# A two-layer hybrid decoder step on one core: the low halves of the second layer's input weights computed on VectorE instead of GpSimd

## The chip, the cores and the metric

The kernel runs on one core of one Trainium2 chip. The metric is the device time of one execution in microseconds (us), the median of three runs. A profile is one further execution, taken by the hardware profiler. Engines are called as the profile calls them: PE is TensorE (matmuls; PEld its weight loads), DVE is VectorE, ACT is ScalarE, POOL is GpSimd, SP is SyncE, which issues all DMAs here. L92 is line 92 of the kernel.

## The reference, cut to what matters

One inference step of a decoder trunk with two layers, for 1024 prompt tokens and 8 sample tokens that share all weights, in float32, model width 1024. The first layer (attention and a state-space scan) is not touched. The second is an mLSTM layer with 8 heads of width 256:

```python
def odd_layer(hn, w_in, w_out, conv_w, conv_b, ig_b, fg_b, norm_w, conv_buf, c0, n0, m0):
    u = hn @ w_in
    q_pre, k_pre, v, o_pre, i_pre, f_pre, z = _split(u, ODD_SPLITS)
    qk, new_conv = causal_conv(jnp.concatenate([q_pre, k_pre], axis=-1), conv_buf, conv_w, conv_b)
    ...
    i_t = i_pre.astype(jnp.float32) + ig_b.astype(jnp.float32)
    logf = jax.nn.log_sigmoid(f_pre.astype(jnp.float32) + fg_b.astype(jnp.float32))
    h, c, n, m = mlstm_chunked(q, k, v, i_t, logf, c0, n0, m0)
    h = jax.nn.sigmoid(o_pre.astype(jnp.float32)).reshape(b, L, MLSTM_HEADS, MLSTM_HD) * h
    h = head_norm(h, norm_w).reshape(b, L, MLSTM_INNER).astype(hn.dtype)
    out = (h * jax.nn.silu(z)) @ w_out
    return out, new_conv, c, n, m
```

`mlstm_chunked` runs over chunks of 128 tokens. For the 8 sample tokens the same layer updates 8 large state matrices (one step each).

## The kernel before, in words

A float32 product is made of three matmuls of a faster 32-bit type (`mm3`, L113): every operand x is split into a high half, which ScalarE casts (`split`, L91), and a low half x minus high, which is one subtraction (L92) on an engine that the call names: `V` is VectorE, `G` is GpSimd. Activations are split once (tiles `yh`, `yl` in the second layer). Weights are split as they stream in: `raw_load` (L96) brings a 128x1024 block from memory into one of three `raw` buffers, `wsplit` makes `wh` and `wl`, or `wvh` and `wvl`, from it.

Two queues of weights feed the second layer's heads:

- `wq1`, a `Weights` object: 48 blocks, six a head, four for q and k and two for the gate z. `next` hands out one block and fetches (cast and subtraction) the next. Its high and low halves have two buffers each, so the cast of a block waits until TensorE has finished the block two places before it. `first` names the engines of the first subtractions, `engs` those of the rest, in turn.
- `wv_fetch`: 32 blocks, four a head, for v and o, which lie ready for the whole head.

A head runs so. For each of the four q and k blocks `conv_c` makes three chunks of 344 columns, 24 matmuls each, in PSUM (`pf`, three banks), and ScalarE copies each out (L238, L240). Then comes the convolution (`conv_taps`: L244 on ScalarE, three L246 on VectorE) and, one block later, its activation (`conv_act`: L250 on ScalarE, L251 on VectorE). For the two z blocks `gate_c` empties a bank with a copy and a tanh on ScalarE (L231, `gth` L232), and VectorE multiplies (L233, `msz`). Between the blocks stand the sample tokens' convolution (L265 to L270 and L277 on VectorE, `csy` and `cst`; L276 on ScalarE) and, from head 2 on, steps of the state update for the sample tokens of the two heads before: a load of `dC` (L1345), a scaling on ScalarE (L1394), then in turn four L1398 (`dC`) and four L1402 (`dnum`) on VectorE, and a store (L1403). An even head has three such steps, an odd head seven. After the z blocks follow nine `vo_block`s with the chunks of the mLSTM (`ml_prep`, `ml_main`, `ml_out`), in which GpSimd has work of its own (`mE`, `mqq`, `mql`, `mCl`, `md`).

In head 0 a chain for the gates runs beside the projections: `lf` and the matmul `pbc` (L1177), a running maximum in seven pairs of steps (`gp`, L1191 and L1192) and the transpose `pgl` (L1197), a recurrence over the eight chunks (`mp`, L1199 and L1200) and the matmul `pmb` (L1207).

After the heads comes the output projection (`wqf`, matmul L927), whose blocks are split on VectorE and GpSimd in turn.

The order of instructions on each engine is set by a scheduler when the program is built; each engine then works through its queue in that order, and one that waits holds up all behind it.

Of the kernel before, what the change touches and what calls it, by code (L numbers as in the profile page):

```python
# [7 lines left out]
F32R = mybir.dt.float32r  # L8
# [21 lines left out]
def body(ctx, tc, I, O):  # L30
    nc = tc.nc
    V, A, G, PE = nc.vector, nc.scalar, nc.gpsimd, nc.tensor
# [4 lines left out]
    def pool(name, bufs=1, stack=ctx, **kw):  # L37
        return stack.enter_context(tc.tile_pool(name=name, bufs=bufs, **kw))
# [18 lines left out]
    def S(name, dt=F32):  # L57
        return cur["slab"].tile([128, 1040], dt, tag="S", name=name)
# [31 lines left out]
    def split(hi, lo, src, eng=V):  # L90
        A.copy(hi, src)  # L91
        eng.tensor_tensor(lo, src, hi.bitcast(F32), sub)  # L92

    def raw_load(src, n):
        raw = rawp.tile([128, 1040], F32, tag="raw", name="raw")
        load(raw[:, :n], src)  # L96
        return raw

    def wsplit(src, n, th, tl, eng=V, raw=None):
        raw = raw_load(src, n) if raw is None else raw  # L100
        split(th[:, :n], tl[:, :n], raw[:, :n], eng)
        return th, tl
# [1006 lines left out]

    layer1 = scope("1", SLABS1)  # L1110
    cur["w"] = pool("wp1", 2, layer1)
    wq1 = Weights([(I[n_][h, j], 1024) for h in range(8) for n_, cnt in (("wq", 4), ("wz", 2)) for j in range(cnt)], (G,), (V, V))

    gb = C("gb", [128, 16], I["gb"].partition_broadcast(128))
    wgr = TMP("wgr")[:, :128].rearrange("p (a b) -> p a b", b=16)
# [315 lines left out]
    wvr = deque()  # L1431

    wvraw = deque()

    def wv_load():
        if wvp and not wvraw:
            wvraw.append(raw_load(I["wvo"][wvp[0][0], wvp[0][1]], 1024))

    def wv_fetch(n):
        for _ in range(n):  # L1440
            wv_load()
            wvp.popleft()
            wvr.append(wsplit(None, 1024, S("wvh", F32R), S("wvl", F32R), G, wvraw.popleft()))

    def vo_block(hd, c, wv):
        p = MM("pvo")
# [49 lines left out]
    for h in range(8):  # L1496
# [3 lines left out]
        for j in range(4):  # L1500
# [24 lines left out]
            if j == 2:  # L1525
                wv_load()
        hd["q"], hd["k"] = qk[0:2], qk[2:4]
        wv_fetch(2)
        hist = SM("mhist", [128, 4, 3, 8], 1)
        load(hist, I["mch"][:, 4 * h : 4 * h + 4])  # L1530
        smp = conv_sample_taps(mxs, hist, mcw[:, 4 * h : 4 * h + 4], mcb[:, 4 * h : 4 * h + 4], 4, O["mconvs"][:, 4 * h : 4 * h + 4])
        hd["z"] = []
        for j in range(2):
            w = wq1.next()
            t2 = S("msz")
            for c in range(3):
                gate_c(w, xh, xl, c, t2[:, c * CH : (c + 1) * CH])
                if j == 0 and c == 2:
                    t = conv_sample_act(*smp)
                slot(c)  # L1540
            A.copy(szs[:, 2 * h + j], t2[:, NP:T])
            hd["z"].append(t2)
            wv_fetch(1)
            if h2 or j == 0:
                pump(1)
# [299 lines left out]
```

## Time and profile before

| | us |
|---|---|
| median of three runs | 2216.33 (2213.23 to 2218.28) |
| the profiled execution | 2213.76 |
| its span, first to last instruction | 2211.7 |
| granted TensorE clock, mean over the span | 0.986 |
| busy PE, DVE, ACT, POOL | 2117.2, 1381.0, 845.4, 857.7 |
| the second layer's heads | about 836 to 2004 of the span |
| the output projection and final norm | 2004 to the end |

Busy time of PE is not PE at its peak: matmuls are pipelined, and at half clock they are busy twice as long. In a row of waits stand the waiting instruction, what ended the wait, the total, the number and the longest. In a timeline row stand start, length and instruction, and in brackets the engine's idle time before it.

### The profile page before, as it was taken

Reading aid. Unit: us, or ns where it says so; the run is one execution under the profiler, and the core shown is the slowest. Engines: PE = TensorE matmul, PEld = TensorE weight load, DVE = VectorE, ACT = ScalarE, POOL = GpSimd, SP = SyncE. Lnnn points to the kernel's source line nnn. Section 1 sums busy time; section 2 is a strip of 40 time slices with the busy share of each in tenths; the row PEclk is TensorE's granted clock in tenths of the full one; section 3 lists DMA queues with packets and bytes.
Section 4 is the critical chain, followed back from the end, with each engine's and each line's share of the span. In section 5 each row is a group of like instructions: output and inputs, shape, how many; then the busy total and the mean of one; then the engine's idle time right before and its main releaser. Section 6 shows DMA issues by size and latency. Waiting matters only on the chain. (4 is left out here: it accounts for less than half of the span.)

```text
span 2211.7 us, 35220 instructions
## 1 busy us (share of the span) xinstructions
PE 2117.2 (96%) x12913; PEld 1890.8 (85%) x12913; DVE 1381.0 (62%) x3075; ACT 845.4 (38%) x1828; POOL 857.7 (39%) x1167
## 2 busy tenths in 40 slices
PE   7999989998999999899999999999999999999998
PEld 6877777997898798789988889898898988987798
DVE  7344488678877545644648566576575664856854
ACT  5434434454434323433424334243343342523331
POOL 4222152115543343343444435434354344542321
PEclk9999999999999999999999999999999999999999
DMA  4222142325555551411213223132241232415753
GB/s 156 70 73 76 52 145 73 93 71 174 166 183 185 159 175 40 94 37 48 88 33 109 77 89 123 36 102 82 75 138 28 84 104 61 139 38 187 256 179 101
DMA packets 161918, 232.29 MB, mean 105 GB/s; under 512 B 41170, under 2 KB 106690, under 8 KB 161746
## 3 DMA queue, kind: packets, MB, share of 16 engines
q1 hardware_dynamic: 161746, 230.04, 33.2%
q8 instruction: 102, 1.67, 0.3%
q14 instruction: 70, 0.57, 0.1%
HBM read 174.35 MB, written 55.62 MB: 104 GB/s over the span
## 5 line engine op out<-in xcount | busy, mean ns | idle before, releaser
L113 PE MATMUL pf<-yh,wh 128*128 128x344 f32 x1152 | 375.5, 326 | 11.9 <-ACT gth L232 11.0
L113 PE MATMUL pf<-yl,wh 128*128 128x344 f32 x1152 | 372.7, 323 | 1.7 <-POOL yl L92 1.7
L113 PE MATMUL pf<-yh,wl 128*128 128x344 f32 x1152 | 371.5, 323 | 0.3 <-DVE wl L92 0.3
L92 POOL TENSOR_TENSOR wl<-raw,wh 128x1024 fp32r<-128x1024 f32 x86 | 214.6, 2495 | 353.6 <-ACT wh L91 353.6
L113 PEld LDWEIGHTS pf<-yh,wh 128*128 128x128 f32 x1152 | 219.6, 191 | 16.6 <-ACT gth L232 13.5
L113 PEld LDWEIGHTS pf<-yl,wh 128*128 128x128 f32 x1152 | 219.6, 191 | 2.6 <-POOL yl L92 2.6
L113 PEld LDWEIGHTS pf<-yh,wl 128*128 128x128 f32 x1152 | 219.2, 190 | 0.8 <-DVE wl L92 0.7
L246 DVE SCALAR_TENSOR_TENSOR cout<-craw,mcw,cout 128x1024 f32<-128x1024 f32 x96 | 145.7, 1518 | 114.7 <-ACT cout L244 113.1
L91 ACT CAST wh<-raw 128x1024 fp32r<-128x1024 f32 x128 | 134.1, 1048 | 207.6 <-PE po L927 82.0
L113 PE MATMUL pvo<-wvh,yh 128*128 128x512 f32 x512 | 205.8, 402 | 0.0
L113 PE MATMUL pvo<-wvl,yh 128*128 128x512 f32 x512 | 201.7, 394 | 0.0
L113 PE MATMUL pvo<-wvh,yl 128*128 128x512 f32 x512 | 201.6, 394 | 0.0
L113 PE MATMUL pf<-xh,wh 128*128 128x344 f32 x576 | 195.8, 340 | 2.7 <-ACT gth L232 2.7
L113 PE MATMUL pf<-xl,wh 128*128 128x344 f32 x576 | 188.0, 326 | 0.0
L113 PE MATMUL pf<-xh,wl 128*128 128x344 f32 x576 | 187.7, 326 | 0.0
L1263 DVE TENSOR_SCALAR mx<-mx,mbs,md 128x256 f32<-128x256 f32 x64 | 26.4, 413 | 178.0 <-POOL md L1262 178.0
L927 PE MATMUL po<-oh,wl 128*128 128x512 f32 (+2 forms) x384 | 123.6, 322 | 5.2 <-DVE wl L92 4.2
L927 PE MATMUL po<-oh,wh 128*128 128x512 f32 (+2 forms) x384 | 123.9, 324 | 1.0 <-ACT oh L91 1.0
L927 PE MATMUL po<-ol,wh 128*128 128x512 f32 (+2 forms) x384 | 123.1, 321 | 0.0
L113 PEld LDWEIGHTS pf<-xh,wh 128*128 128x128 f32 x576 | 110.8, 192 | 8.8 <-issue 4.9
L92 POOL TENSOR_TENSOR wvl<-raw,wvh 128x1024 fp32r<-128x1024 f32 x32 | 85.5, 2674 | 78.1 <-ACT wvh L91 78.1
L113 PEld LDWEIGHTS pvo<-wvh,yl 128*128 128x128 f32 x512 | 96.1, 188 | 22.3
(435 smaller groups left out, 5307.0 us busy)
## 6 DMA issues: line engine op xcount, KB each, us to landing
raw<-in_wo SPq DMA_DIRECT2D x56, 512.0 KB
raw<-in_wq SPq DMA_DIRECT2D x32, 512.0 KB
raw<-in_wvo SPq DMA_DIRECT2D x32, 512.0 KB
dC<-in_mcs SPq DMA_DIRECT2D x32, 512.0 KB
out_mcs<-dC SPq DMA_DIRECT2D x32, 512.0 KB
raw<-in_wf SPq DMA_DIRECT2D x24, 512.0 KB
sE<-acd SPq DMA_DIRECT2D x16, 512.0 KB
raw<-in_wz SPq DMA_DIRECT2D x16, 512.0 KB
```

The source lines that it names most:

```text
L91: A.copy(hi, src)
L92: eng.tensor_tensor(lo, src, hi.bitcast(F32), sub)
L113: PE.matmul(out, l, r, start=i == 0, stop=i == n - 1)
L246: V.scalar_tensor_tensor(o[:, :NP], raw[:, j : j + NP], w4[:, j : j + 1], o[:, :NP], mult, add)
L927: PE.matmul(p[:, :m], wt[:, ws], at, start=i == 0 and q == 0, stop=i == nk - 1 and q == 2)
L1263: V.tensor_scalar(x, x, bs[:, 6:7], d[:, 2:3], sub, mult)
```

## The change

The subtractions of the low halves of `wq1` and of the value weights name VectorE. The first two of `wq1` did so before; 46 of `wq1` and 32 of `wv_fetch` move. The output projection's blocks (`wqf`) still take VectorE and GpSimd in turn.

```diff
     cur["w"] = pool("wp1", 2, layer1)
-    wq1 = Weights([(I[n_][h, j], 1024) for h in range(8) for n_, cnt in (("wq", 4), ("wz", 2)) for j in range(cnt)], (G,), (V, V))
+    wq1 = Weights([(I[n_][h, j], 1024) for h in range(8) for n_, cnt in (("wq", 4), ("wz", 2)) for j in range(cnt)], (V,))
...
         for _ in range(n):
             wv_load()
             wvp.popleft()
-            wvr.append(wsplit(None, 1024, S("wvh", F32R), S("wvl", F32R), G, wvraw.popleft()))
+            wvr.append(wsplit(None, 1024, S("wvh", F32R), S("wvl", F32R), V, wvraw.popleft()))
```

The scheduler places the moved subtractions in VectorE's queue and moves some neighbours. First place: VectorE in head 4, at the fourth k block, where the sample convolution (L268 to L277) stands ahead of the first z block; + is after, - before.

```order
+L92 TENSOR_TENSOR wl<-raw,wh 128x1024
 L268 TENSOR_TENSOR cst<-mxs,mcw 128x32
 L269 TENSOR_TENSOR csy<-csy,cst 128x32
 L270 TENSOR_TENSOR csy<-csy,mcb 128x32
 L246 SCALAR_TENSOR_TENSOR cout<-craw,mcw,cout 128x1024
+L92 TENSOR_TENSOR wvl<-raw,wvh 128x1024
+L246 SCALAR_TENSOR_TENSOR cout<-craw,mcw,cout 128x1024
+L92 TENSOR_TENSOR wvl<-raw,wvh 128x1024
+L246 SCALAR_TENSOR_TENSOR cout<-craw,mcw,cout 128x1024
+L233 SCALAR_TENSOR_TENSOR msz<-gth,msz 128x344 x2
 L277 SCALAR_TENSOR_TENSOR cst<-cst,csy 128x32
```

The weight's subtraction comes ahead of L268, and two value subtractions come between the three L246 of that block; the other q and k blocks have their subtraction ahead of their three L246.

Second place: ScalarE in the same stretch of head 1, at the first z block (the other heads up to 6 read alike).

```order
 L232 ACTIVATE gth<-pf 128x344
-L250 ACTIVATE craw<-cout 128x1024
-L231 COPY msz<-pf 128x344
-L232 ACTIVATE gth<-pf 128x344
-L91 CAST wvh<-raw 128x1024
+L231 COPY msz<-pf 128x344
+L232 ACTIVATE gth<-pf 128x344
+L91 CAST wvh<-raw 128x1024
+L250 ACTIVATE craw<-cout 128x1024
 L91 CAST wh<-raw 128x1024
```

L250, which waits for the third L246 on VectorE, now comes behind the second copy and tanh of the z block.

Third place: VectorE in head 0, inside the running maximum `gp`.

```order
+L92 TENSOR_TENSOR wl<-raw,wh 128x1024
 L1191 TENSOR_TENSOR gp<-gp 64x124
 L1192 COPY gp<-gp 64x4
-L268 TENSOR_TENSOR cst<-mxs,mcw 128x32
+L246 SCALAR_TENSOR_TENSOR cout<-craw,mcw,cout 128x1024
 L1191 TENSOR_TENSOR gp<-gp 64x120
 L1192 COPY gp<-gp 64x8
-L269 TENSOR_TENSOR csy<-csy,cst 128x32
+L246 SCALAR_TENSOR_TENSOR cout<-craw,mcw,cout 128x1024
```

A subtraction and three L246 (before, these stood behind or at the end of `gp`) come into the chain, and a value subtraction ahead of its last pair. On TensorE the transpose `pgl` stands 5 matmuls later than before, and `pmb` 57 matmuls behind `pgl` instead of 31.

## The prediction

> **What bounds the kernel now.** I read the page first, then the windows of the second layer's part, the waits of TensorE there, the groups of VectorE and GpSimd, and last the timeline at the longest waits. Page, the busy row:
>
> ```profile
> PE 2117.2 (96%) x12913; PEld 1890.8 (85%) x12913; DVE 1381.0 (62%) x3075; ACT 845.4 (38%) x1828; POOL 857.7 (39%) x1167
> ```
>
> TensorE is the bound. The windows (columns: stretch, length, busy of PE, PEld, DVE, ACT, POOL, granted clock, DMA share, GB/s) give the eight heads of the second layer, one heavy and one light slice of them, and four stretches at half clock:
>
> ```profile
> 836.00:2004.00 1168.00, 1135.74 (x6653) 1032.16 (x6653) 712.82 (x1653) 434.51 (x900) 522.71 (x780) 0.99 0.25 78
> 1480.00:1500.00 20.00, 17.69 (x101) 17.12 (x101) 18.16 (x21) 11.28 (x18) 9.95 (x5) 0.91 0.36 119
> 1940.00:1960.00 20.00, 20.00 (x109) 16.87 (x108) 9.63 (x37) 6.36 (x18) 6.59 (x15) 1.00 0.07 18
> 912.30:915.70 3.40, 2.99 (x11) 2.88 (x12) 3.40 (x7) 0.33 (x1) 0.28 (x1) 0.51 0.43 154
> 922.60:929.40 6.80, 4.29 (x16) 4.14 (x17) 3.45 (x21) 1.06 (x4) 0.20 (x1) 0.50 0.37 129
> 1492.60:1496.00 3.40, 3.40 (x14) 3.40 (x13) 3.40 (x3) 0.00 (x0) 2.36 (x1) 0.50 0.05 8
> 1779.30:1782.70 3.40, 3.40 (x14) 3.40 (x13) 3.40 (x4) 0.07 (x1) 0.83 (x1) 0.50 0.85 306
> ```
>
> TensorE is short of work for 32 of the 1168 us, and where it is, VectorE is nearly full (18.16 of 20). So TensorE's time can only fall by its waits and by the half clock behind them. Its waits in that part (total, times, longest):
>
> ```profile
> PE pf L113 <- ACT gth L232: 11.0, 9, 2.2
> PE pmb L1207 <- DVE mp L1200: 5.8, 1, 5.8
> PE pgl L1197 <- DVE gp L1191: 3.4, 1, 3.4
> PE pbc L1177 <- DVE lf L295: 1.2, 1, 1.2
> PE pf L113 <- ACT craw L238: 1.0, 2, 0.8
> ```
>
> These 22.4 us come from VectorE: directly in the gate chain (mp, gp, lf: 10.4), and through ScalarE in the projections (12.0), because ScalarE's queue stands still on VectorE's results before it empties a PSUM bank. The timeline at the first wait of 2.2 us (start, length, instruction; brackets: idle before):
>
> ```profile
> 1197.71 2.40 POOL L92 TENSOR_TENSOR wl<-raw,wh 128x1024 fp32r<-128x1024 f32 x1 [5.66 <-ACT wh L91]
> 1197.76 2.63 DVE L1402 SCALAR_TENSOR_TENSOR dnum<-dC,dq,dnum 128x256 f32<-128x256 f32 x1
> 1200.31 3.04 DVE L1398 SCALAR_TENSOR_TENSOR dC<-dvb,dkw,dC 128x256 f32<-128x256 f32 x2
> 1200.45 2.62 POOL L92 TENSOR_TENSOR wvl<-raw,wvh 128x1024 fp32r<-128x1024 f32 x1
> 1204.63 0.19 DVE L270 TENSOR_TENSOR csy<-csy,mcb 128x32 f32<-128x32 f32 x1
> 1204.86 0.23 ACT L276 ACTIVATE cst<-csy 128x32 f32<-128x32 f32 x1 [4.62 <-DVE csy L270]
> 1206.78 0.43 PE L113 MATMUL pf<-yh,wh 128*128 128x344 f32 x1 [2.23 <-ACT gth L232]
> ```
>
> A VectorE instruction of half a microsecond lasts 2.6 us, as long as the GpSimd subtraction that it meets. That is the rule, not this spot: the groups (count, busy, mean ns) and, behind them, min/median/max ns of the same instructions:
>
> ```profile
> L92 POOL TENSOR_TENSOR wl<-raw,wh 128x1024 fp32r<-128x1024 f32 x47 | 117.3, 2496 | 155.3 <-ACT wh L91 155.3
> L92 POOL TENSOR_TENSOR wvl<-raw,wvh 128x1024 fp32r<-128x1024 f32 x32 | 85.5, 2674 | 78.1 <-ACT wvh L91 78.1
> L246 DVE SCALAR_TENSOR_TENSOR cout<-craw,mcw,cout 128x1024 f32<-128x1024 f32 x96 | 145.7, 1518 | 114.7 <-ACT cout L244 113.1
> L1402 DVE SCALAR_TENSOR_TENSOR dnum<-dC,dq,dnum 128x256 f32<-128x256 f32 x93 | 67.3, 724 | 0.7
> L1398 DVE SCALAR_TENSOR_TENSOR dC<-dvb,dkw,dC 128x256 f32<-128x256 f32 x96 | 64.1, 701 | 13.5 <-ACT dC L1394 13.2
> L233 DVE SCALAR_TENSOR_TENSOR msz<-gth,msz 128x344 f32<-128x344 f32 x48 | 50.9, 1063 | 40.4 <-ACT gth L232 40.4
> ```
> ```profile
> L246 DVE SCALAR_TENSOR_TENSOR cout<-craw,mcw,cout x96: 1270/1285/3498, 872.6 to 1920.4; 128x1024 f32<-128x1024 f32 x96
> L1402 DVE SCALAR_TENSOR_TENSOR dnum<-dC,dq,dnum x93: 469/480/2664, 1170.5 to 1916.8; 128x256 f32<-128x256 f32 x93
> L1398 DVE SCALAR_TENSOR_TENSOR dC<-dvb,dkw,dC x96: 469/480/2652, 1169.1 to 1913.8; 128x256 f32<-128x256 f32 x96
> L233 DVE SCALAR_TENSOR_TENSOR msz<-gth,msz x48: 471/516/2749, 915.2 to 1936.9; 128x344 f32<-128x344 f32 x48
> L92 DVE TENSOR_TENSOR wl<-raw,wh x3: 1203/1214/1218, 837.1 to 1927.8; 128x1024 fp32r<-128x1024 f32 x3
> ```
>
> **The change part by part.** Taken off GpSimd: 46 subtractions of projection weights (one of the 47 above is the output projection's and stays) at 2.496 us and 32 of value weights, 85.5 us: 200 us. It was no bound (523 of 1168 us busy), so this alone gives nothing.
>
> Put on VectorE: 78 subtractions at 1.214 us, 94.7 us. Given back there, mean minus median times count: L246 22.4, L1402 22.7, L1398 21.2, L233 26.3, together 92.6 us, and some 11 us more from five small gate instructions, each held about 2.2 us:
>
> ```profile
> 903.49 2.59 DVE L1192 COPY gp<-gp 64x8 f32<-64x8 f32 x1
> 906.11 2.62 DVE L1191 TENSOR_TENSOR gp<-gp 64x112 f32<-64x112 f32 x1
> 910.30 2.35 DVE L1191 TENSOR_TENSOR gp<-gp 64x64 f32<-64x64 f32 x1
> 918.21 2.32 DVE L1200 TENSOR_TENSOR mp<-mp,btot 1x8 f32<-1x8 f32 x1
> 920.75 2.07 DVE L1200 TENSOR_TENSOR mp<-mp,btot 1x8 f32<-1x8 f32 x1
> ```
>
> VectorE's load so stays where it is (about -9 us); what changes is where its time falls. A subtraction now stands directly behind the cast that it needs and ahead of the three L246, which wait for ScalarE's L244 (113.1 us of idle time): it fills a pause where VectorE is early.
>
> Whether TensorE then waits for the subtraction itself: the weight is needed one weight later, 72 matmuls (three chunks of 24) after the cast may start; the chain has a stretch without a wait:
>
> ```profile
> 1868.37 18.75 PE pf L113 x119
> ```
>
> That is 0.157 us for one, 11.3 us for 72; cast and subtraction take 2.3. VectorE may be 9 us behind before it costs anything. Queued behind the waiting subtraction are L246 and the dC steps; SyncE waits for it too, since the raw buffer is then free for the next load, which comes sooner by 1.2 us where VectorE is not late. DMA counts do not change.
>
> Projection waits, at 1204: 2.15 us of L1402 and 2.16 of the two L1398 go, 1.21 is added, so L270 ends 3.1 us earlier than the 2.2 us wait needs. Moreover L250, on which ScalarE also stood, is now behind the second gth. I take 9 of the 12.0 us.
>
> Gate chain: between the start of gp and its end 6.8 us of holding go, and two subtractions and three L246 come in (2.4 + 3.9): 0.5 us earlier, and TensorE asks for it 5 matmuls (0.8 us) later. The mp chain loses 4.1 us of holding and, ahead of it, two L246, and gets two subtractions and one L233; it ends some 3 us earlier, and TensorE asks 31 matmuls (4.9 us) later. I take 7 of the 10.4 us: pmb nearly all, pgl 1.3, pbc the rest.
>
> Half clock: in the four stretches TensorE is busy 14.1 us at half speed, so 7.0 us are lost; each comes shortly after a wait. I take 4. By the Trainium skill, "TensorE: Matmul & The Clock Gate", section "Why this matters for your kernels", the clock drops after TensorE gaps above about 3 us; the trace does not agree for 1492.6 and 1779.3, where no wait on a bank is longer than 2.2 us. By that rule these two would stay, and the sum would be about 2 us smaller.
>
> New waits: bounds 0 and the rival's 25 us; I take 2, since the 9 us of slack are near the first.
>
> Sum: 9 + 7 + 4 - 2 = 18 us off the profiled execution's 2213.76 (span 2211.7, 2.1 around it): 2195.8. The median of the runs is 2216.33, 2.6 above that execution, so I say 2198. All of 22.4 + 7.0 gone would give 2184 to 2187.
>
> **The rivals.** Slower: the subtraction comes too late. VectorE works in order; in a head's heavy weights it has L246 three times (3.86), L251 (1.22, from the row below), eight dC and dnum steps (3.84), one subtraction (1.21) and two thirds of a value one (0.81): 10.9 of 11.3 us. Above 11.3 it falls behind with every weight. One such wait stands in the output projection, where the subtraction is on VectorE behind the same steps:
>
> ```profile
> PE po L927 <- DVE wl L92: 4.2, 1, 4.2
> L251 DVE SCALAR_TENSOR_TENSOR cout<-craw,cout 128x1024 f32<-128x1024 f32 x32 | 39.1, 1223 | 13.0 <-ACT craw L250 13.0
> ACT dC L1394 <- DMA dC<-in_mcs: 55.4, 16, 5.8
> ```
>
> Once in each of the six heads with such steps is 25 us, less the 20: 2221. Against it: in every second head only two of the four q and k weights carry steps, and a z weight with one (three L233 1.5, steps 3.84, subtractions 2.0: 7.4 us) leaves 4 us to catch up.
>
> No change: ScalarE then stands on the loads of dC instead (last row, 16 times), the banks are emptied as late as now, and of the gate chain only pmb's later place counts: minus 3, 2213. Against it: L276 and L250 waited for VectorE, not for a load, where TensorE stood.
>
> Halfway: the gate chain's 7 us come, the projection waits stay: 2209.
>
> The Trainium skill, "SBUF — State Buffer", section "Who interferes with whom", speaks against the change in one point: a VectorE instruction with two SBUF inputs and a GpSimd one that reads SBUF exclude each other, so a moved subtraction can now be held by what stays on GpSimd. By it, at 28% of GpSimd's time left (322 of 1168) and an estimated 0.7 us each, 15 us come back onto VectorE; the row of L92 on VectorE above (three of them, at most 1.218) does not show it. They would be hidden by the same slack.
>
> **How the numbers follow.** Forecast 0.62 (its own range 2190 to 2206), halfway 0.15 (2206 to 2211), no change 0.12, slower 0.11. Less than 0.2% (4.4 us) cannot be told from no change: faster 0.77, same 0.12, slower 0.11. From all gained (2183) up to the middle of no change (2216) lie about 8 in 10.
>
> **What would show it.** The medians stay and the maxima of L246, L1402, L1398 and L233 fall below 2 us, VectorE's busy time in the heads stays within 20 us of 713, GpSimd's falls to about 320; the waits on gth and pmb are nearly gone, as are the half-clock stretches after 900. A row in which pf waits for VectorE's wl, or ScalarE waiting for a load of raw ahead of gth, would make the forecast wrong; so would a gate chain that ends as late as now.

## The result and the profile after

| | before | after |
|---|---|---|
| median, same chip | 2215.74 us (2213.23 to 2218.28) | 2180.67 us (2178.78 to 2186.08) |
| ratio | 1 | 0.9842, 95% interval 0.9823 to 0.9860 |
| profiled execution | 2213.76 us, span 2211.7 | 2182.44 us, span 2180.5 |

The change takes 35 us off; 18 were forecast, and the range ended at 2183. The page's busy row of the changed kernel:

```profile
PE 2104.4 (97%) x12913; PEld 1884.0 (86%) x12913; DVE 1356.9 (62%) x3153; ACT 847.8 (39%) x1828; POOL 665.8 (31%) x1089
```

VectorE has 78 more instructions of 1.2 us and is busy 24 us less. The windows (same columns as before): the heads, a heavy slice, and the one stretch at half clock that is left there, at the start of the heads, where before had one as well:

```profile
840.00:1972.00 1132.00, 1122.80 (x6653) 1024.55 (x6652) 687.36 (x1731) 437.21 (x900) 334.34 (x702) 1.00 0.26 80
1443.00:1463.00 20.00, 20.00 (x130) 20.00 (x129) 16.95 (x25) 11.30 (x18) 6.68 (x10) 1.00 0.40 125
841.00:847.80 6.80, 6.32 (x23) 5.10 (x22) 3.94 (x10) 0.01 (x1) 4.71 (x11) 0.50 0.13 25
```

TensorE is short of work for 9 us of the 1132 in place of 32 of 1168. Its waits from 848 on name none of the five causes of before:

```profile
PE mH L1336 <- DVE mx L1263: 3.7, 7, 1.0
PE mN L113 <- POOL mCl L92: 2.2, 3, 1.0
PE pf L113 <- POOL yl L92: 2.1, 3, 0.9
```

The instructions that were held, and the moved subtractions (min/median/max ns), then the groups with their means, two of the gate chain's among them:

```profile
L246 DVE SCALAR_TENSOR_TENSOR cout<-craw,mcw,cout x96: 1267/1284/1310, 875.6 to 1889.7; 128x1024 f32<-128x1024 f32 x96
L1402 DVE SCALAR_TENSOR_TENSOR dnum<-dC,dq,dnum x93: 473/480/962, 1159.1 to 1882.9; 128x256 f32<-128x256 f32 x93
L1398 DVE SCALAR_TENSOR_TENSOR dC<-dvb,dkw,dC x96: 471/479/691, 1157.6 to 1882.0; 128x256 f32<-128x256 f32 x96
L233 DVE SCALAR_TENSOR_TENSOR msz<-gth,msz x48: 471/510/777, 914.1 to 1905.0; 128x344 f32<-128x344 f32 x48
L92 DVE TENSOR_TENSOR wl<-raw,wh x49: 1201/1225/1490, 841.0 to 1895.2; 128x1024 fp32r<-128x1024 f32 x49
L92 DVE TENSOR_TENSOR wvl<-raw,wvh x32: 1205/1220/1227, 910.2 to 1898.7; 128x1024 fp32r<-128x1024 f32 x32
```
```profile
L246 DVE SCALAR_TENSOR_TENSOR cout<-craw,mcw,cout 128x1024 f32<-128x1024 f32 x96 | 123.1, 1283 | 8.3 <-ACT cout L244 6.8
L92 DVE TENSOR_TENSOR wl<-raw,wh 128x1024 fp32r<-128x1024 f32 x49 | 61.5, 1255 | 93.7 <-ACT wh L91 93.6
L1191 DVE TENSOR_TENSOR gp<-gp 64x127 f32<-64x127 f32 (+6 forms) x7 | 1.8, 258 | 0.1
L1200 DVE TENSOR_TENSOR mp<-mp,btot 1x8 f32<-1x8 f32 x8 | 1.2, 152 | 0.2
```

The medians stand as before (1285, 480, 480, 516); the maxima of 2.6 to 3.5 us are gone. And the pause has changed its name: VectorE waited 113.1 us for ScalarE's L244 ahead of L246 and now waits 6.8; it waits 93.6 for the casts ahead of the subtractions. The moved work stands in VectorE's old idle time. The place of the timeline that the prediction showed, one weight of head 2, with its steps, its subtraction and the last of the sample taps:

```profile
1181.92 0.88 DVE L1398 SCALAR_TENSOR_TENSOR dC<-dvb,dkw,dC 128x256 f32<-128x256 f32 x2
1182.71 1.00 DVE L1402 SCALAR_TENSOR_TENSOR dnum<-dC,dq,dnum 128x256 f32<-128x256 f32 x2
1183.63 1.22 DVE L92 TENSOR_TENSOR wl<-raw,wh 128x1024 fp32r<-128x1024 f32 x1
1185.21 0.19 DVE L270 TENSOR_TENSOR csy<-csy,mcb 128x32 f32<-128x32 f32 x1
```

Two L1402 take 1.00 us where one took 2.63, and from the start of these two to that of L270 there are 2.5 us.

Where the time went, by the first TensorE row of the heads (prb) and the rows of the value projections (first and last start behind the durations), before and then after:

```profile
L203 PE MATMUL prb<-dg,ones x10: 357/421/582, 839.5 to 843.8; 128*128 128x128 f32 x8, 8*128 8x8 f32 x2
L113 PE MATMUL pvo<-wvh,yh x512: 387/393/507, 938.3 to 1994.3; 128*128 128x512 f32 x171
```
```profile
L203 PE MATMUL prb<-dg,ones x10: 330/421/580, 843.4 to 847.7; 128*128 128x128 f32 x8, 8*128 8x8 f32 x2
L113 PE MATMUL pvo<-wvh,yh x512: 387/393/508, 927.4 to 1962.4; 128*128 128x512 f32 x171
```

Head 0's projections and the gate chain went from 98.8 to 84.0 us (14.8 less), the rest of the heads from 1056.0 to 1035.0 (21.0 less): 35.8 us. These two stretches are called head 0 and the later heads below; their lengths in other runs are read from the same two rows. In this execution the first layer, which is the same code, took 3.9 us longer and the tail 0.7, so that the profiled executions lie 31.3 apart and the medians 35.

### The profile page after: what moved, and what is told of

It is laid out like the page before. It is cut to its first block, busy times and chain, and to the rows that moved or that the text cites. A ratio compares the mean times of both kernels' runs of the same rounds, so it can differ in the third digit from the quotient of the medians.

```text
span 2180.5 us, 35187 instructions
## 1 busy us (share of the span) xinstructions
PE 2104.4 (97%) x12913; PEld 1884.0 (86%) x12913; DVE 1356.9 (62%) x3153; ACT 847.8 (39%) x1828; POOL 665.8 (31%) x1089
## 4 chain that ended last, share of the span: by engine, by line
PE 56%; DVE 3%; POOL 2%; DMA 2%; issue 1%; ACT 1%; POOLq 0%; DVEq 0%; SPq 0%; ACTq 0%
PE pf L113 24%; PE pvo L113 16%; PE po L927 8%; PE mN L113 2%; PE mC L113 2%; PE mS L1275 1%; DMA dC<-in_mcs 1%; POOL mCl L92 1%; PE mH L1336 1%; PE mS L1277 1%; DVE dnum L1402 0%; DVE dC L1398 0%; DMA mE<-mud 0%; POOL md L1261 0%; PE prb L203 0%
## 5 line engine op out<-in xcount | busy, mean ns | idle before, releaser
L113 PE MATMUL pf<-yh,wh 128*128 128x344 f32 x1152 | 371.0, 322 | 0.0
L92 DVE TENSOR_TENSOR wl<-raw,wh 128x1024 fp32r<-128x1024 f32 x88 | 111.6, 1268 | 133.7 <-ACT wh L91 133.5
L92 POOL TENSOR_TENSOR wl<-raw,wh 128x1024 fp32r<-128x1024 f32 x40 | 99.3, 2483 | 220.0 <-ACT wh L91 220.0
L246 DVE SCALAR_TENSOR_TENSOR cout<-craw,mcw,cout 128x1024 f32<-128x1024 f32 x96 | 123.1, 1283 | 8.3 <-ACT cout L244 6.8
```

What stands on the lines that cost most here:

```text
L113: PE.matmul(out, l, r, start=i == 0, stop=i == n - 1)
L246: V.scalar_tensor_tensor(o[:, :NP], raw[:, j : j + NP], w4[:, j : j + 1], o[:, :NP], mult, add)
```

## The experiments

Every experiment was timed in five rounds beside the kernel before; gains are (1 - ratio) x 2216 us. The theories: T1, VectorE's instructions with two inputs in SBUF no longer stand still beside GpSimd's subtractions; T2, the low halves are ready sooner; T3, the new order of the instructions. Lines added to a kernel shift its line numbers (msz is L236 or L238 in some rows).

| run | median us | ratio to before, 95% | against before |
|---|---|---|---|
| after | 2180.67 | 0.9842 (0.9823 to 0.9860) | -35 us |
| wl alone moved | 2190.34 | 0.9884 (0.9870 to 0.9897) | -26 |
| wvl alone moved | 2192.72 | 0.9892 (0.9876 to 0.9908) | -24 |
| every second one moved | 2192.78 | 0.9881 (0.9866 to 0.9896) | -26 |
| before, in quarters | 2207.90 | 0.9963 (0.9951 to 0.9976) | -8 |
| after, subtraction again on GpSimd | 2273.06 | 1.0252 (1.0236 to 1.0268) | +56 |
| after, one-input operation, 1024 columns | 2201.12 | 0.9926 (0.9908 to 0.9944) | -16 |
| the same, 860 columns | 2195.24 | 0.9894 (0.9878 to 0.9911) | -23 |
| after, memset of raw | 2189.52 | 0.9881 (0.9867 to 0.9894) | -26 |
| after, free memset, one | 2189.21 | 0.9878 (0.9863 to 0.9894) | -27 |
| after, free memset, long | 2224.54 | 1.0037 (1.0021 to 1.0054) | +8 |
| after, subtraction twice on VectorE | 2197.82 | 0.9916 (0.9899 to 0.9933) | -19 |
| after, no low halves | 2176.58 | 0.9818 (0.9803 to 0.9834) | -40 |
| after, 14 slabs | 2180.50 | 0.9839 (0.9826 to 0.9852) | -36 |
| after, wo0 too | 2174.34 | 0.9808 (0.9794 to 0.9822) | -43 |
| after, all weights | 2173.50 | 0.9806 (0.9792 to 0.9819) | -43 |
| wo0, mCl, mql, mqq too | 2168.80 | 0.9785 (0.9766 to 0.9804) | -48 |
| those and all weights | 2171.99 | 0.9790 (0.9775 to 0.9804) | -47 |

**One part alone: the projections' weights (e1).**

```diff
-    wq1 = Weights([...], (G,), (V, V))
+    wq1 = Weights([...], (V,))
```

> The kernel before with one part of the change alone: the subtractions of wq1 (tile wl) go to VectorE, those of wv_fetch (tile wvl) stay on GpSimd. Theory T1 (VectorE's instructions with two SBUF inputs were held while a GpSimd subtraction of 2.4 us read SBUF): about two thirds of the lost VectorE time in the trace of before lies beside wl, a third beside wvl, so two thirds of the 35 us: about 2193 us, with msz<-gth still seen over 2 us beside wvl. T2 (the low half is ready in 1.2 us in place of 2.5 and the raw buffer is free sooner): no wait of the profile names wvl, so wl brings nearly all: about 2182 us. T3 (the scheduler's new order brings it): 2181 if the order of wl's heads matters, else 2215; no size in between follows from it.

Measured 2190.34 us, 26 of the 35, near T1's figure. Two of its waits of TensorE, and the gate product, still held beside wvl:

```profile
PE pgl L1197 <- DVE gp L1191: 4.4, 1, 4.4
PE pf L113 <- ACT gth L232: 3.2, 3, 1.2
L233 DVE SCALAR_TENSOR_TENSOR msz<-gth,msz x48: 472/510/2687, 913.8 to 1914.5; 128x344 f32<-128x344 f32 x48
```

**The other part alone: the value weights (e2).**

```diff
-            wvr.append(wsplit(None, 1024, ..., G, wvraw.popleft()))
+            wvr.append(wsplit(None, 1024, ..., V, wvraw.popleft()))
```

> The kernel before with the other part alone: the subtractions of wv_fetch (tile wvl) go to VectorE, 46 of the 48 of wq1 stay on GpSimd. T1: a third of the 35 us, about 2204 us, and the sum of this gain and of the one with wq1 alone is about 35 us. T2: 2214 to 2216 us, no change. T3: no change, 2215 us.

Measured 2192.72, 24 us of gain. No wait on gth is left, though the subtractions of wq1, whose product TensorE needs there, are still on GpSimd; what is left of the five causes is pmb and 1.2 us on lf:

```profile
PE pmb L1207 <- DVE mp L1200: 3.7, 1, 3.7
L233 DVE SCALAR_TENSOR_TENSOR msz<-gth,msz x48: 471/510/2504, 920.7 to 1918.6; 128x344 f32<-128x344 f32 x48
```

T2 and T3 expected nothing of this run, and it gave two thirds; that counts against both. But T1's shares failed too: 26 and 24 add up to 50, not 35. The lengths say where: in head 0 the two parts add up (90.7 and 92.2 us, so 8.1 and 6.6 of the 14.8 less), while in the later heads either part brings most of the 21.0 (1038.7 and 1035.4 us, so 17.3 and 20.6). There either part takes away much of the same waits.

**Every second one (e15).**

```diff
-    wq1 = Weights([...], (G,), (V, V))
+    wq1 = Weights([...], (V, G))
+    wveng = iter((V, G) * 16)
-            wvr.append(wsplit(None, 1024, ..., G, wvraw.popleft()))
+            wvr.append(wsplit(None, 1024, ..., next(wveng), wvraw.popleft()))
```

> The kernel before with every second subtraction of wq1 and of wv_fetch on VectorE, so that 40 of the 80 stay on GpSimd (before: 78). If each hold costs its share: half of the 35.6 us, 2198 us, and the gains of the two parts alone (26 and 24 us) would be an accident of which were moved. If the time is lost only where holds pile up beyond what VectorE can catch up (so that either part alone brings two thirds): 2186 to 2192 us, with msz<-gth still seen over 2 us but TensorE's wait on gth below 5 us.

Measured 2192.78, 26 us of gain with 40 of the 80 still on GpSimd; proportional would be 17.5. By the ratio that is clear of proportion (0.9921 is outside 0.9866 to 0.9896), by the median 0.8 us above the band for piling up. The wait on gth is gone altogether, with msz<-gth still held up to 2.2 us; besides pmb, pgl is late again by 1.3 us:

```profile
PE pmb L1207 <- DVE mp L1200: 3.3, 1, 3.3
L233 DVE SCALAR_TENSOR_TENSOR msz<-gth,msz x48: 470/511/2168, 921.7 to 1917.3; 128x344 f32<-128x344 f32 x48
```

The later heads take 1034.9 us, as after (1035.0), though L1398 still lasts up to 2.65 us; in e2 its mean is even that of before (700 ns, before 701). So in the later heads single holds cost little: VectorE makes them up before TensorE needs the result. That time is lost where several follow one another, as in the timeline at 1197 to 1203 us of before, fits this, but no run tests it by itself. Moving 32, 39, 46 and 78 subtractions gains 24, 26, 26 and 35 us.

**Shorter holds (e4).** The kernel before, each GpSimd subtraction in four pieces; nothing moves.

```diff
+        for j in range(pieces):
+            js = slice(j * n // pieces, (j + 1) * n // pieces)
+            eng.tensor_tensor(tl[:, js], raw[:, js], th[:, js].bitcast(F32), sub)
...
+    wq1.pieces = 4
```

> The kernel before with every GpSimd subtraction of wq1 and wv_fetch cut into four of 256 columns; nothing moves to VectorE. T1, if VectorE gets in between two pieces: no hold is longer than about 0.65 us in place of 2.45, so about three quarters of the gain: 2189 us, and msz<-gth at most some 1.2 us. T1, if it does not get in between: 2215 us and still over 2 us. T2: 2215 us or a little more (the low half is ready no sooner). T3: 2215 us, its order on VectorE and ScalarE is that of before but for a few rows.

Measured 2207.90: 8 us of gain, not 26. T2 and T3 expected none, so a length of hold does count; but a piece of 256 columns takes 0.74 us where a quarter of 2.43 is 0.61, and there are four of them for VectorE to meet:

```profile
L104 POOL TENSOR_TENSOR wvl<-raw,wvh x128: 713/742/1732, 917.8 to 1928.3; 128x256 fp32r<-128x256 f32 x128
L237 DVE SCALAR_TENSOR_TENSOR msz<-gth,msz x48: 472/523/1056, 913.3 to 1929.0; 128x344 f32<-128x344 f32 x48
L250 DVE SCALAR_TENSOR_TENSOR cout<-craw,mcw,cout x96: 1269/1651/1869, 878.0 to 1914.7; 128x1024 f32<-128x1024 f32 x96
```

The maximum is 1.06 us, as T1 said. But now the median of L246 (L250 here) is 1.65 in place of 1.28: more than half of them are held a little, and its mean of 1605 ns is above the 1518 of before. The gain is head 0's (89.6 us); the later heads, at 1053.0, are almost as long as before (1056.0).

**The reads put back (e3).** The changed kernel, and GpSimd subtracts a second time into a scratch tile. A slab is one buffer of the kernel's working memory; one fewer makes room for that tile.

```diff
-SLABS1 = 15
+SLABS1 = 14
...
+        G.tensor_tensor(junk, raw[:, :1024], th[:, :1024].bitcast(F32), sub)
```

> The changed kernel with its subtractions on VectorE, and each of the 80 done a second time on GpSimd into a scratch tile that nothing reads (one slab fewer, 14 for 15, makes room for it). The low halves are as early as after the change and TensorE's order is row for row that of the changed kernel; only GpSimd's reads of SBUF are back. T1: the loss comes back: 2208 to 2222 us, above before where the moved subtractions, which have two SBUF inputs themselves, are now held too; VectorE's longest msz<-gth over 2 us again. T2: 2181 to 2184 us (the raw buffers alone come free later). T3: 2181 us, the order of the changed kernel.

Measured 2273.06 us, 92 above after and beyond the band of T1:

```profile
PE pf L115 <- ACT gth L235: 31.7, 11, 4.6
L236 DVE SCALAR_TENSOR_TENSOR msz<-gth,msz x48: 472/506/2744, 929.5 to 1998.2; 128x344 f32<-128x344 f32 x48
L92 DVE TENSOR_TENSOR wl<-raw,wh x49: 1201/1226/3448, 840.0 to 1990.0; 128x1024 fp32r<-128x1024 f32 x49
L1119 POOL TENSOR_TENSOR junk<-raw,wh x48: 2327/3238/3512, 840.3 to 1978.8; 128x1024 f32<-128x1024 f32 x48
```

Now the moved subtraction is held as well (up to 3.4 us), and GpSimd's own lasts 3.24 us at the median in place of 2.43: the two engines stop each other. TensorE's order is that of the changed kernel, so T3 falls as the only cause: this order alone does not bring the time. The Trainium skill, "SBUF — State Buffer", section "Who interferes with whom", says that a VectorE instruction with two inputs in SBUF contends with a GpSimd instruction that reads SBUF; the trace agrees where GpSimd has two inputs, and the next two runs show much shorter holds where it has one.

**GpSimd busy, without two inputs (e12, e14).** At the same 80 places of the program GpSimd multiplies the raw tile by 1.0 into the scratch tile, in all 1024 columns and then in 860, which last about as long as a subtraction. The multiplication needs only the raw tile, so it starts when the load has landed (GpSimd's idle time before it ends with the load) and not, as the subtraction, behind the cast.

```diff
+        G.tensor_scalar(junk, raw[:, :1024], 1.0, None, mult)
```

> The changed kernel, and at each of the 80 places a GpSimd multiplication of the raw tile by 1.0 into a scratch tile (one input from SBUF in place of the subtraction's two; 14 slabs). If any read of GpSimd holds VectorE: a loss in the measure of its length, 2215 to 2270 us, with msz<-gth beyond 1.5 us. If only its instructions with two SBUF inputs do: 2181 to 2192 us, as with one memset. T2 expects 2181 to 2185 in either case (raw buffers a little later).

> As the run with the multiplication by 1.0 (2201 us), with 860 columns in place of 1024, so that GpSimd is kept busy for about 2.4 us at each of the 80 places, as with the subtraction before the change (2.42 to 2.43 us), and holds VectorE little. What it lies above the changed kernel's 2181 us is then the part of the change's 35 us that comes from GpSimd's time and its single-input reads; what it lies below before is the part of the two-input holds. T1, with the holds for nearly all: 2181 to 2190 us. Half and half: 2190 to 2205. GpSimd's own queue for nearly all: over 2205 us.

Measured 2201.12, between its two bands, and 2195.24, in the middle one of three. The 1024 columns first, then the 860:

```profile
L1119 POOL TENSOR_SCALAR junk<-raw x80: 2769/2869/4271, 839.9 to 1911.3; 128x1024 f32<-128x1024 f32 x80
L236 DVE SCALAR_TENSOR_TENSOR msz<-gth,msz x48: 470/510/949, 919.4 to 1922.6; 128x344 f32<-128x344 f32 x48
```
```profile
L1119 POOL TENSOR_SCALAR junk<-raw x80: 2360/2564/3749, 840.8 to 1905.4; 128x860 f32<-128x860 f32 x80
L236 DVE SCALAR_TENSOR_TENSOR msz<-gth,msz x48: 470/510/1227, 920.9 to 1917.4; 128x344 f32<-128x344 f32 x48
```

With 860 columns GpSimd is busy longer than with the subtraction of before (2.56 against 2.43), somewhat earlier, and 23 of the 35 us stay gained: so about two thirds of the gain are VectorE's holds by two-input instructions. An operation with one input holds VectorE too, msz<-gth at most for 0.4 and 0.7 us and the gate chain's mp (L1209) for 1.05 and 0.73 us (1202 and 881 ns in place of 153), not for the operation's whole length.

**GpSimd busy in its places without reads (e18, with e17).** After each subtraction GpSimd sets the raw tile to zero, for 2.43 us in all; and the changed kernel with one slab fewer, as a control for the runs with a scratch tile.

```diff
+            G.memset(raw[:, :1024], 0.0)
+            G.memset(raw[:, :1024], 0.0)
+            G.memset(raw[:, :512], 0.0)
```

> The changed kernel, and after each of the 80 subtractions GpSimd sets the raw tile to zero in three memsets (1024, 1024 and 512 columns, about 2.43 us, 15 slabs). In the earlier memset runs nothing held the memsets to their places, and all 80 ran early (838.7 to 937.2 us, and 845.9 to 1110.6 us); here each must wait for its subtraction and the next load for it, so GpSimd is busy for a subtraction's time at its place, and reads nothing. If the 11 to 20 us of the one-input runs are GpSimd's time in its queue: 2190 to 2200 us, with TensorE's waits on mCl, mql and mx longer. If they are single-input reads that hold VectorE: 2179 to 2187 us. A raw buffer that is free later by 2.4 us could add loads that come late: then waits on wh or raw.

> The changed kernel with one slab fewer (14 for 15) and nothing else: it says how much of the runs with a scratch tile is the slab. Expected by every theory: 2178 to 2184 us, since the run with no low halves at 14 slabs was at 2177. If 2186 or more, that much comes off the price of GpSimd's time.

Measured 2189.52 and 2180.50; the slab costs nothing. The memset run:

```profile
L103 POOL MEMSET raw<- x80: 941/953/962, 842.9 to 1905.8; 128x1024 f32 x80
L238 DVE SCALAR_TENSOR_TENSOR msz<-gth,msz x48: 472/511/602, 919.1 to 1912.1; 128x344 f32<-128x344 f32 x48
PE pgl L1203 <- DVE gp L1197: 4.1, 1, 4.1
L117 PE MATMUL pvo<-wvh,yh x512: 387/393/507, 935.0 to 1969.4; 128*128 128x512 f32 x171
```

Of the later heads nothing is lost: they take 1034.4 us, as after (1035.0), though GpSimd is as busy at the moved subtractions as before and the raw buffers come free later. So there neither of the two counts. The time is 9 us above after, and of the 7.5 us between the two profiled spans 7.1 stand in head 0 (91.1 us), where the gate chain is late again. Two things are seen there. ScalarE's cast for the subtraction ahead of gp's third step comes 5 us later than after (908.1, after 903.1); the trace doesn't show why. And msz is held no more (602 ns at most), but VectorE's instructions with one input are, for as long as a memset lasts:

```profile
910.52 1.08 DVE L1198 COPY gp<-gp 64x4 f32<-64x4 f32 x1
910.63 0.95 POOL L103 MEMSET raw<- 128x1024 f32 x1
```

So about 26 us of the 35 go with VectorE's holds by GpSimd's two-input reads; the 9 stand in head 0, and how they divide between later raw buffers, such held copies and GpSimd's time stays open. The time fits neither of the expected bands.

**Two runs that missed their aim (e6, e10).** The changed kernel with one memset, then with three, of a scratch tile.

> The changed kernel, and at each of the 80 places a GpSimd memset of 128x1024 into a scratch tile that nothing reads (14 slabs): GpSimd is kept busy in its queue at the same places as where the subtraction was done a second time (2273 us), but reads no SBUF and frees no raw buffer later. T1 (the reads hold VectorE): 2179 to 2186 us, and VectorE's msz<-gth and cout<-craw stay below 0.9 and 1.4 us. If it is GpSimd's queue (mCl, yl, qk and gates behind longer work) or any access of GpSimd to SBUF that costs the time: 2200 us or more, in the measure of the memset's length.

> The changed kernel, and at each of the 80 places three GpSimd memsets into a scratch tile (1024, 1024 and 512 columns, about 0.95 + 0.95 + 0.48 us by the memset run), so that GpSimd is kept busy for the 2.4 us of a subtraction and reads nothing (14 slabs). The second subtraction at these places gave 2273 us, one memset 2189. T1 with the reads as the cause: 2190 to 2215 us, what is lost shows as TensorE waiting for GpSimd's own results (mql, mCl, yl), and VectorE's cout<-craw and msz<-gth have no instruction over 1.4 and 0.9 us. If GpSimd's time alone is the cause: 2250 us or more, as with the second subtraction.

Measured 2189.21 and 2224.54, each between its two bands. These memsets have no input, and the scheduler put all of them early, so they do not stand at the subtractions' places:

```profile
L1119 POOL MEMSET junk<- x80: 942/954/978, 845.9 to 1110.6; 128x1024 f32 x80
PE mH L1347 <- DVE mx L1274: 15.7, 11, 1.9
```

What they show is what a full GpSimd queue does: 80 x 2.43 = 194 us of the 265 are filled, mx waits for GpSimd's md, and TensorE for mx. For the change's gain they prove nothing.

**The later low half, on VectorE (e11).** Each subtraction twice in a row into the same tile.

```diff
+            eng.tensor_tensor(tl[:, :n], raw[:, :n], th[:, :n].bitcast(F32), sub)
```

> The changed kernel, with each of the 80 subtractions done twice in a row on VectorE into the same tile: the low half is ready after about 2.45 us, as late as GpSimd made it before, the raw buffer comes free as late, VectorE has 98 us more work, and GpSimd has none of it. T1: 2179 to 2186 us. T2 (the later low half and raw buffer were the cost): 2210 us or more. If VectorE has no room for it, the time rises too, and the waits of TensorE then name VectorE's results (gth, mp, mx) with no VectorE instruction longer than after the change.

Measured 2197.82: 17 us above after, below T2's band and above T1's.

```profile
PE pmb L1211 <- DVE mp L1204: 4.3, 1, 4.3
L236 DVE SCALAR_TENSOR_TENSOR msz<-gth,msz x48: 472/510/519, 923.6 to 1921.2; 128x344 f32<-128x344 f32 x48
```

The gate product is not held (519 ns at most), and no wait of TensorE in the projections names wl or gth; the longest is the gate chain's in head 0, and the only one that names a moved low half is 0.7 us for wvl. Of the 15.5 us between the two profiled spans 12.2 stand in head 0 (96.2 us) and 2.9 in the later heads (1037.9). That speaks for VectorE's queue rather than for the late low half, but one run doubles both, so a part for T2 is not excluded; in the later heads it is 2.9 us at most.

**No subtraction at all (e5).** One tile of zeros stands for all low halves of wq, wz and wvo.

> The changed kernel without the 80 subtractions: the low halves of wq, wz and wvo in the second layer are left out, one tile of zeros stands for all of them (one slab fewer, 14), and TensorE still does every matmul. It takes 80 x 1.22 = 98 us off VectorE and gives GpSimd nothing. T1, with the holds as the whole cost: 2176 to 2182 us, since the waits that are left in the heads name mx, mCl and yl. If the subtractions cost something on VectorE after all (a late wl, a VectorE too full), the time falls below 2172, and the fall is that cost. T2: the low half is then there at once, so some us below 2181, 2175 or less.

Measured 2176.58, 4 us below after, within T1's band and above T2's; the intervals of the two overlap. So the 98 us of subtraction cost some 4 us on VectorE. The next 98 (e11) cost 17.

**Further on the same way (e9, e8, e13, e16).** The subtractions of wo0, then of all weights; then wo0's with the low halves of the state and of q (mCl, mql) and the product mqq; then both.

> The changed kernel with the 24 subtractions of wo0 (first layer's output, 678 to 827 us) on VectorE as well. T1: VectorE lost some 20 us there beside GpSimd's subtractions of 2.4 us; TensorE stood 2.9, 3.4, 1.4 and 2.2 us there (647, 722, 740 and 837 us), behind the sums of squares for the most part; a part of it goes: 2174 to 2180 us. T2 (the low half sooner): 2181, no wait there names wl. If VectorE is the bound of that stage, 24 x 1.22 = 29 us more on it: 2185 to 2200.

> The changed kernel with every subtraction of a weight on VectorE, those of w1 and wo0 of the first layer and of wo1 at the end too; GpSimd keeps its other work. T1: the gain of wo0 alone and some us of the waits on acc, PT, P and sbt in the first layer (8.6, 7.1, 5.6, 5.7 us in all), of which GpSimd's other instructions (dk, dv, dso, xl) hold the larger part: 2166 to 2178 us. At the end (1980 to 2160 us) nothing: TensorE waited 4.2 us for one wl of VectorE there, which may become more. If VectorE is too full in the first layer: 2182 to 2200.

> The run with wo0 on VectorE too (2174 us), and the state's and q's low halves (mCl, mql) and the product mqq on VectorE as well: GpSimd's last long instructions with two SBUF inputs in the heads are gone, VectorE has about 56 x (0.6 + 0.35) + 112 x 0.2 = 75 us more. T1: the waits on mCl (2.5 us) and part of those on mx (4.6 us) and the VectorE time lost beside mCl go: 2166 to 2174 us. If VectorE's queue is now too full: 2176 to 2190 us, with waits that name mCl or mql from VectorE.

> The fastest run so far (2169 us: wo0, mCl, mql and mqq on VectorE too), with the subtractions of w1 and of wo1 on VectorE as well. T1: w1 and wo1 brought 1 us within the interval when moved beside wo0, so 2165 to 2170 us; slower than 2171 if VectorE at the start (0 to 60 us) or at the end (1980 to 2160 us) has no room.

Measured 2174.34, 2173.50, 2168.80 and 2171.99; the first three lie in T1's bands, the last 2 us above its own. With wo0 moved, the sums of squares ahead of the heads are free as well; after (first row) and the run with wo0:

```profile
L213 DVE TENSOR_TENSOR ssdst<-ssdst,sq x14: 691/700/2457, 707.9 to 838.9; 128x512 f32<-128x512 f32 x7, 128x520 f32<-128x520 f32 x7
```
```profile
L213 DVE TENSOR_TENSOR ssdst<-ssdst,sq x14: 674/693/700, 709.4 to 833.2; 128x512 f32<-128x512 f32 x7, 128x520 f32<-128x520 f32 x7
```

The weights w1 and wo1 add nothing that the intervals can tell. The fastest version by its median is the third:

```profile
L1402 DVE SCALAR_TENSOR_TENSOR dnum<-dC,dq,dnum x93: 476/480/489, 1147.2 to 1863.6; 128x256 f32<-128x256 f32 x93
```

Its ratio of 0.9785 against 0.9842 is some 13 us below the change as it was made. With all of GpSimd's long two-input work gone, L1402 has no held instruction at all (489 ns at most).

## Why the prediction was wrong in size

The mechanism was right: the holds, the absence of a price on TensorE's path, the waits that go. What failed is the sum, in four terms: three discounts on what the trace listed, and one price for waits that did not come.

**Projection waits, 9 of 12.0.** All went: after has no row on gth or craw. The step reckoned at one place what VectorE gains there (3.1 us) and took a discount for the others. The runs with one part moved show why no discount was due: half of the holds taken away, or fewer, already ends every wait on gth (e2, e15); with wl alone moved 3.2 us of it stay (e1).

**Gate chain, 7 of 10.4.** All went, pgl too, of which 2.1 us were kept back because two subtractions and three L246 stand ahead now. They do, but gp's steps are 258 ns on average in place of 906, as the row of before has it, and pgl is in time:

```profile
L1191 DVE TENSOR_TENSOR gp<-gp 64x127 f32<-64x127 f32 (+6 forms) x7 | 6.3, 906 | 0.1
```

Where one kind stays on GpSimd, pgl or pmb come back (4.4 and 3.7 us). The new order has its part here, as the prediction had reckoned: after, mp ends at 920.45, 8.9 us behind pgl's start at 911.60, and 57 matmuls of 0.157 us are 8.9 us; at the old distance of 31 (4.9 us) TensorE would have waited some 4 us by this estimate. No run has the old order without the holds, so T3 is excluded as the only cause, not as a part of the gain.

**Half clock, 4 of 7.0.** All four stretches went, and one more that the sum did not count:

```profile
854.30:857.70 3.40, 3.21 (x11) 2.77 (x12) 2.40 (x6) 1.15 (x5) 2.10 (x5) 0.50 0.04 10
```

That is 17.3 us of busy time at half speed, 8.6 lost by the prediction's halving. (In the trace the matmuls of pf start 0.287 us apart there and 0.157 elsewhere, so it is nearer 7.8.) By the rule of the Trainium skill, "TensorE: Matmul & The Clock Gate", section "Why this matters for your kernels", those at 1492.6 and 1779.3 would have stayed, since no gap there is above 3 us; they went with the waits of 1.9 and 2.2 us ahead of them, so here the trace does not bear that rule out. Nor does every such wait bring one: behind two others of before, 2.2 us at 1206.8 and 1.9 at 1212.7, the clock stays at 1.00.

**New waits, minus 2.** None came: from 848 us on no row of TensorE's waits names a moved wl or wvl. The slower rival, a subtraction more than 9 us late, did not come even with twice the work on VectorE (e11). ScalarE waits 40.4 us for loads of dC in place of 55.4, so the rival of no change fell too:

```profile
ACT dC L1394 <- DMA dC<-in_mcs: 40.4, 15, 5.9
```

With all of it, 22.4 + 8.6 = 31.0 of the 35.8 us in the heads; so the fast end of the range, which was all listed terms gone, had no room for what the rows did not list. In head 0 the account closes to within 0.8: 10.4 + 5.2 (the half-clock stretches at 854, 912 and 922) against 14.8 measured. In the other heads it is 12.0 + 3.4 against 21.0. A part of the 5.6 is a habit of the view: a matmul of pf is shown 0.32 us long and the next starts 0.16 us after it, so each of the 11 listed waits is shown about 0.16 us short (1.8 us). By the starts of the matmuls the value projections of heads 2, 4 and 6 are 0.7 to 1.0 us shorter each (2.4 us). Some 1.4 us stay unassigned.

The rule of the Trainium skill's "SBUF — State Buffer" on shared reads was priced at 15 us on VectorE, hidden: its condition is real (e3), but beside what stayed on GpSimd the moved wl came to (1255 - 1220) x 49 = 1.7 us.

What stays open: how the 9 us of e18, all in head 0, divide, whether the late low half has any part in e11's 17, and how much the new order brings beside the holds, in head 0 above all.

## What to carry to other kernels

When an instruction's maximum is several times its median, ask what runs beside it on another engine before asking whether its own engine is full: here a VectorE busy 61% of the heads took in 95 us more work and finished earlier. Where a trace shows such waits with one cause, and the change takes the cause away, forecast all of them and the clock behind them, since holds that follow one another make the wait, and the first ones removed bring most of it. A control that keeps an engine busy needs a dependency that holds it in place, or the scheduler moves it.

## What the runs showed of the hardware that was not expected

- The standstill is mutual: GpSimd's two-input subtraction took 3.24 us at the median in place of 2.43 where VectorE's stood beside it, and VectorE's up to 3.45 in place of 1.22 (e3).
- A GpSimd multiplication with one input (2.87 us for 128x1024) held VectorE's msz<-gth for at most 0.4 us (0.7 us in the run with 860 columns) and mp for at most 1.05, and it lasts longer than the subtraction with two (2.43 us).
- VectorE's copies, which have one input, stand still as well: gp (L1192) took 2.59 us beside GpSimd's subtraction in before, and 1.08 beside a memset of 0.95 us (e18), in place of 0.15. The two-input msz is not held by a memset (602 ns at most).
- A 128x256 piece of the subtraction takes 0.74 us on GpSimd, so four cost 2.97 us against 2.43.
- Half clock followed two of the four TensorE waits of 1.9 to 2.2 us in the later heads of before, and left with them.
